# A column roll from memory to memory: both rows of a DMA engine in one transfer, and rings that take blocks in turn

## The chip, the core and the metric

The kernel runs on one core of a Trainium2 chip. The metric is the device time of one execution in microseconds (us); the time of a kernel is the median of its runs. The core has 16 DMA engines that all its DMA queues share, and five instruction engines. Three of these issue DMAs here: SP (SyncE) and ACT (ScalarE), each with a hardware ring, and POOL (GpSimd), with a software queue.

## The reference

```python
def setup_inputs():
    return {"x": np.random.randn(8192, 8192).astype(np.float32), "shift": 100}

def reference(x, shift):
    return np.roll(x, shift, axis=1)
```

Each of 8192 rows of 8192 float32 numbers (32 KB) is turned to the right by 100 places. Column c of the output is column c - 100 of the input; the first 100 columns of the output are the last 100 of the input. Nothing is computed: 268 MB are read and 268 MB are written.

## The kernel before

With `s = 100`, the kernel rounds the shift up to `a = 128` columns and cuts each row in two. The long part, output columns 128 to 8191, comes from input columns 28 to 8091. It goes from memory to memory in one step (line 36). The short part, output columns 0 to 127, goes through the core's own memory (lines 48 to 68).

The long part is cut into 256 blocks of 32 rows (lines 27 to 36). A block is seen as `e = 16` pairs of rows with `j = 2` rows in each, so that DMA engine e is meant to handle the neighbouring rows 2e and 2e + 1 of a block. For every block the kernel starts one DMA with the rows j = 0 on SP's ring and one with the rows j = 1 on ACT's ring. A DMA holds 16 pieces, one for each engine, and a piece is 8064 numbers, 32256 bytes. In the last eight blocks the columns are cut at `mid = 4096`, and each ring gets two DMAs per block, with pieces of 3968 and 4096 numbers. Each ring carries 248 + 16 = 264 DMAs.

The framework that schedules the program gives each ring four completion semaphores in turn. The order of instructions with their waits shows it: the first four DMAs of a ring wait for nothing, and each later one waits until the DMA four places ahead of it has landed in full, from all 16 engines. So a ring has at most four DMAs in flight. SP and ACT have no other work.

The short part is done in 16 groups of 512 rows. POOL loads each group with three DMAs (lines 60, 61 and 64), DVE copies the pieces into place (lines 62 and 65), and at the end POOL stores the 16 groups (line 68). POOL has eight completion semaphores in turn, so it has at most eight DMAs in flight. No row of the output is written twice and nothing in the long part waits for the short part or the other way round; they share the 16 DMA engines and the memory.

Of the kernel before, what the change touches and what calls it, by code (L numbers as in the profile page):

```python
# [1 line left out]

# [4 lines left out]


@with_exitstack
def kernel(  # L10
    ctx: ExitStack,
    tc: tile.TileContext,
    x: bass.AP,
    shift: int,
    out: bass.AP,
):
    nc = tc.nc
    n_rows, n_cols = x.shape
    s = shift % n_cols
    a = -(-s // 128) * 128  # L20
    g = a - s
    P = nc.NUM_PARTITIONS
    engines = [nc.sync, nc.scalar]
    n_chunks = 16
    rows = n_rows // n_chunks

    xm = x.rearrange("(c e j) w -> c j e w", e=16, j=2)
    om = out.rearrange("(c e j) w -> c j e w", e=16, j=2)
    if a < n_cols:
        blocks = n_rows // 32  # L30
        mid = (a + n_cols) // 256 * 128
        for c in range(blocks):
            parts = ((a, mid), (mid, n_cols)) if c >= blocks - 8 and a < mid else ((a, n_cols),)
            for j in range(2):
                for lo, hi in parts:
                    engines[j].dma_start(out=om[c, j, :, lo:hi], in_=xm[c, j, :, lo - s:hi - s])
    if a == 0:
        return

    if a > 512:  # L40
        for i in range(n_chunks):
            r = slice(i * rows, (i + 1) * rows)
            nc.gpsimd.dma_start(out=out[r, :s], in_=x[r, n_cols - s:])
            if g > 0:
                nc.gpsimd.dma_start(out=out[r, s:a], in_=x[r, :g])
        return

    Q = 4
    n_st = n_rows // (P * Q)
    reads = ctx.enter_context(tc.tile_pool(name="reads", bufs=n_st))  # L50
    heads = ctx.enter_context(tc.tile_pool(name="heads", bufs=n_st))
    xt = x.rearrange("(k p q) c -> k p q c", q=Q, p=P)
    ot = out.rearrange("(k p q) c -> k p q c", q=Q, p=P)
    tiles = []
    for k in range(n_st):
        t = reads.tile([P, Q - 1, a], x.dtype)
        h = heads.tile([P, Q, a], x.dtype)
        lead = bass.AP(tensor=x.tensor, offset=(k * P * Q + 1) * n_cols - s,
                       ap=[[Q * n_cols, P], [n_cols, Q - 1], [1, a]])
        nc.gpsimd.dma_start(out=t[:], in_=lead, single_packet=True)  # L60
        nc.gpsimd.dma_start(out=h[:, Q - 1, :s], in_=xt[k, :, Q - 1, n_cols - s:], single_packet=True)  # L61
        nc.vector.tensor_copy(h[:, :Q - 1, :s], t[:, :, :s])  # L62
        if g > 0:
            nc.gpsimd.dma_start(out=h[:, 0, s:], in_=xt[k, :, 0, :g], single_packet=True)  # L64
            nc.vector.tensor_copy(h[:, 1:, s:], t[:, :, s:])  # L65
        tiles.append(h)
    for k, h in enumerate(tiles):
        nc.gpsimd.dma_start(out=ot[k, :, :, :a], in_=h[:], single_packet=True)  # L68


# [1 line left out]
_INS = ['x', 'shift']  # L72
_OUTS = [((8192, 8192), 'float32')]

_NUMBERS = {'shift': 100}


# [26 lines left out]
```

## Time and profile before

| | |
|---|---|
| time before, median of 3 runs | 827.04 us (826.43 to 828.41) |
| the profiled execution, its own time | 825.38 us |
| its span, first to last instruction | 823.6 us |
| busy: DVE, POOL | 7.8 us (1%), 41.1 us (5%) |
| moved by the DMA engines | 272.71 MB, mean 331 GB/s |
| packets of the DMA engines | 20229, of them 9472 under 512 B |
| DMAs of line 36, per ring | 248 of 504 KB, 8 of 256 KB, 8 of 248 KB |

The page cuts the span into 40 slices. A digit is the share of the slice in tenths in which the 16 DMA engines were busy on average (9 is 90% or more), and below it stand the GB/s that they moved. A queue's line gives its packets, its megabytes and the time of its packets as a share of 16 engines' time. A line for DMA issues gives the number of DMAs, the KB of each, and the median time from issue to landing. In the table of windows, a row has the stretch, its length, the busy time of the engines that worked, the granted clock, the share in which the DMA engines were busy, and GB/s. A line of waits has the total time waited, the number of waits and the longest.

### The profile page before, as it was taken

The page shows a single profiled execution, that of the slowest core. Times are in us where ns is not written, and L with a number is a line of the kernel's source. Part 1 is how long each engine was busy: PE and PEld are TensorE (multiplying, and loading weights), DVE is VectorE, ACT ScalarE, POOL GpSimd, SP SyncE. Part 2 cuts the span into 40 slices and gives each one's busy share as a digit, 9 for nine tenths or more (in the row PEclk, how much of TensorE's full clock was granted, in tenths as well). Part 3 has the DMA queues.
Part 4 walks back from the last instruction along what each step waited for, and adds up shares of the span by engine and source line. Part 5 has one row for each costly group of instructions (what it writes and reads, how often), then busy time and mean ns, then how long its engine had stood idle before and what let it go on. Part 6 is the DMA issues. An engine that isn't in the chain of part 4 may idle for free. (4 is left out here: it accounts for less than half of the span.)

```text
span 823.6 us, 689 instructions
## 1 busy us (share of the span) xinstructions
DVE 7.8 (1%) x32; POOL 41.1 (5%) x68
## 2 busy tenths in 40 slices
DVE  0000000000000000000000000000000000000000
POOL 3111111211100000000000000000000000000000
DMA  9999999999999999999999999999999999999998
GB/s 300 345 338 345 325 338 340 332 344 359 341 341 345 338 337 323 332 332 321 329 331 331 324 329 331 332 326 329 332 326 329 336 323 337 320 335 337 321 312 302
DMA packets 20229, 272.71 MB, mean 331 GB/s; under 512 B 9472, under 2 KB 9728, under 8 KB 11776
## 3 DMA queue, kind: packets, MB, share of 16 engines
q1 hardware_dynamic: 8448, 132.14, 47.8%
q10 hardware_dynamic: 8448, 132.14, 46.7%
q0 software_dynamic: 3328, 8.39, 4.7%
q14 instruction: 5, 0.04, 0.0%
HBM read 268.44 MB, written 268.44 MB: 652 GB/s over the span
## 5 line engine op out<-in xcount | busy, mean ns | idle before, releaser
L68 POOL DMA_DIRECT2D out_dram<-h x16 | 11.4, 712 | 83.1 <-DMA out_dram<-h 49.6
L60 POOL DMA_DIRECT2D t<-in_x_dram x16 | 12.1, 758 | 32.5 <-DMA h<-in_x_dram 31.6
L64 POOL DMA_DIRECT2D h<-in_x_dram x16 | 8.6, 539 | 80.4 <-DMA t<-in_x_dram 80.4
L61 POOL DMA_DIRECT2D h<-in_x_dram x16 | 8.9, 558 | 20.8 <-DMA h<-in_x_dram 20.8
L62 DVE COPY h<-t 128x300 f32<-128x300 f32 x16 | 5.9, 368 | 179.7 <-DMA t<-in_x_dram 179.7
L65 DVE COPY h<-t 128x84 f32<-128x84 f32 x16 | 3.2, 201 | 0.0
L85 POOL MEMSET const-float32-0.0<- 128x1 f32 x1 | 0.1, 99 | 0.2 <-issue 0.2
L85 POOL MEMSET const-bfloat16-1.0<- 128x1 bf16 x1 | 0.1, 101 | 0.0
L85 POOL MEMSET const-uint8-127<- 128x1 uint8 x1 | 0.1, 99 | 0.0
L85 POOL MEMSET const-float32-1.0<- 128x1 f32 x1 | 0.1, 98 | 0.0
## 6 DMA issues: line engine op xcount, KB each, us to landing
out_dram<-in_x_dram ACTq DMA_DIRECT2D x248, 504.0 KB, 12.6
out_dram<-in_x_dram SPq DMA_DIRECT2D x248, 504.0 KB, 12.6
out_dram<-h POOLq DMA_DIRECT2D x16, 256.0 KB, 64.9
t<-in_x_dram POOLq DMA_DIRECT2D x16, 192.0 KB, 31.6
out_dram<-in_x_dram ACTq DMA_DIRECT2D x8, 256.0 KB, 6.0
out_dram<-in_x_dram SPq DMA_DIRECT2D x8, 256.0 KB, 5.9
out_dram<-in_x_dram ACTq DMA_DIRECT2D x8, 248.0 KB, 6.1
out_dram<-in_x_dram SPq DMA_DIRECT2D x8, 248.0 KB, 6.1
```

The lines of the kernel that those rows point to most:

```text
L60: nc.gpsimd.dma_start(out=t[:], in_=lead, single_packet=True)
L61: nc.gpsimd.dma_start(out=h[:, Q - 1, :s], in_=xt[k, :, Q - 1, n_cols - s:], single_packet=True)
L62: nc.vector.tensor_copy(h[:, :Q - 1, :s], t[:, :, :s])
L64: nc.gpsimd.dma_start(out=h[:, 0, s:], in_=xt[k, :, 0, :g], single_packet=True)
L65: nc.vector.tensor_copy(h[:, 1:, s:], t[:, :, s:])
L68: nc.gpsimd.dma_start(out=ot[k, :, :, :a], in_=h[:], single_packet=True)
L85: nc = _bacc.Bacc("TRN2", target_bir_lowering=False, num_devices=1)
```

## The change

Up to block 247, a block goes in one DMA on one ring: 32 pieces, both rows of each engine. Even blocks go on SP's ring and odd blocks on ACT's. In the last eight blocks, each ring carries one DMA per block with one whole piece per engine, SP those with j = 0 and ACT those with j = 1; the cut at `mid` is gone. The order of instructions on the engines shows 124 DMAs of 32 x 8064 and then 8 of 16 x 8064 on each ring, 132 in all. The four semaphores in turn per ring remain. The instructions of POOL and DVE are the same as before.

```diff
-    xm = x.rearrange("(c e j) w -> c j e w", e=16, j=2)
-    om = out.rearrange("(c e j) w -> c j e w", e=16, j=2)
+    xm = x.rearrange("(c e j) w -> c e j w", e=16, j=2)
+    om = out.rearrange("(c e j) w -> c e j w", e=16, j=2)
     if a < n_cols:
         blocks = n_rows // 32
-        mid = (a + n_cols) // 256 * 128
         for c in range(blocks):
-            parts = ((a, mid), (mid, n_cols)) if c >= blocks - 8 and a < mid else ((a, n_cols),)
-            for j in range(2):
-                for lo, hi in parts:
-                    engines[j].dma_start(out=om[c, j, :, lo:hi], in_=xm[c, j, :, lo - s:hi - s])
+            if c < blocks - 8:
+                engines[c % 2].dma_start(out=om[c, :, :, a:], in_=xm[c, :, :, a - s:n_cols - s])
+            else:
+                for j in range(2):
+                    engines[j].dma_start(out=om[c, :, j, a:], in_=xm[c, :, j, a - s:n_cols - s])
```

## The prediction

> **What bounds the kernel now.** I read the page first: its slices, its DMA queues and its memory line.
>
> ```profile
> DMA  9999999999999999999999999999999999999998
> GB/s 300 345 338 345 325 338 340 332 344 359 341 341 345 338 337 323 332 332 321 329 331 331 324 329 331 332 326 329 332 326 329 336 323 337 320 335 337 321 312 302
> q1 hardware_dynamic: 8448, 132.14, 47.8%
> q10 hardware_dynamic: 8448, 132.14, 46.7%
> q0 software_dynamic: 3328, 8.39, 4.7%
> HBM read 268.44 MB, written 268.44 MB: 652 GB/s over the span
> ```
>
> The 16 DMA engines are busy from the first slice to the last, and DVE and POOL work for 1% and 5% of the span. q1 and q10 are the rings of SP and ACT, q0 is POOL's. A ring shows 8448 packets for 264 DMAs: 264 x 16 = 4224 pieces and as many 4-byte packets that report completion.
>
> Second, the DMA view of the middle, 300 to 700 us, where POOL is done, and the instructions of line 36 in the same stretch:
>
> ```profile
> q1 hardware_dynamic: 4077, 65.78, 50.3%
> q10 hardware_dynamic: 4077, 65.75, 49.5%
> out_dram<-in_x_dram SPq DMA_DIRECT2D x128, 504.0 KB, 12.6
> out_dram<-in_x_dram ACTq DMA_DIRECT2D x128, 504.0 KB, 12.6
> ```
> ```profile
> L36 SPq DMA_DIRECT2D out_dram<-in_x_dram x128: 509/510/510, 299.9 to 699.6; - x128
> DMA to landing us min/median/max: 11.6/12.6/13.5
> ```
>
> The shares sum to 99.8%, and the software and instruction queues bring it to 99.9%: no engine goes hungry. One piece with its completion packet takes 0.503 x 16 x 400 us / (4077 / 2) = 1.58 us. A ring has four DMAs in flight (its fifth waits for the first), and 4 x 2 rings x 1.58 = 12.6 us, the landing time exactly. So a DMA's landing time is queueing, and a fixed cost in it would be covered by the seven others.
>
> Third, SP's own waits in that stretch:
>
> ```profile
> SPq L36 <- DMA out_dram<-in_x_dram: 335.3, 128, 3.5
> ```
>
> SP issues for 128 x 0.51 = 65 us and waits 335 us of 400: issuing has five times the room it needs.
>
> What is full then? From 0 to 250 us the DMA view gives 38.45 + 38.65 MB on the two rings and 7.20 MB on POOL's. A ring's byte uses memory twice (read and write), a POOL byte once: (154.2 + 7.2) MB / 250 us = 646 GB/s. In the middle it is 131.53 x 2 / 400 = 658 GB/s. The rate of the DMAs falls from 337 to 329 GB/s when POOL's share goes, while the memory's flow stays within 2%. I take the memory's flow as the bound; the engines are busy because packets wait inside them.
>
> Last, the end, in windows (length, DVE, POOL, clock, DMA share, GB/s):
>
> ```profile
> 600.00:780.00 180.00, 0.00 (x0) 0.00 (x0) 1.00 1.00 330
> 780.00:800.00 20.00, 0.00 (x0) 0.00 (x0) 1.00 0.97 322
> 800.00:810.00 10.00, 0.00 (x0) 0.00 (x0) 1.00 0.91 318
> 810.00:824.00 14.00, 0.00 (x0) 0.00 (x0) 1.00 0.81 269
> ```
>
> The halved pieces run here. Four half-size DMAs per ring are less cover, so 3% and 9% idle appear, and the last 14 us lose 14 x (1 - 269/330) = 2.6 us against the middle's rate.
>
> **The change part by part.**
>
> *Half the DMAs in the bulk.* Each ring issues 124 DMAs of 32 pieces and 8 of 16, 132 in place of 264; bytes are the same. An engine handles 264 completion packets in place of 528 over both rings, and its 32 half pieces of the last blocks become 16 whole ones. What is a completion packet worth? The last stage shows it, since there every 16 KB has one in place of every 32 KB. By elapsed time, 780 to 800 us gives 32256 x 16 / 322 = 1603 ns per 32256 bytes of an engine, the middle 32256 x 16 / 330 = 1564 ns: 39 ns for one more completion, if the whole loss is put on it. By busy time it is 1603 x 0.97 = 1555 ns against 1564: nothing, or below nothing. So the saving is 0 to 264 x 39 ns = 10.3 us. I take 0, by the busy-time row: the 3% is idle time, which a dearer packet would not make.
>
> *Deeper rings.* Four DMAs in flight are now eight pieces per ring and engine in place of four. It can only remove idle time; the middle has 0.1% of it: 0 to 780 x 0.001 = 0.8 us. I take -0.4.
>
> *Rows dealt differently.* Before, the rings work on odd and even rows of one block, 32 KB apart; after, on neighbouring blocks, 1 MB apart. Order on a ring is row 2e, then 2e + 1, of its block for engine e, if the queue deals rows out as the diff's view says. No row depends on another, and nothing else is queued on SP or ACT. Every engine still holds one packet at a time in its own region of memory, and engines already stand at different points of different blocks. I price it at 0 and keep both signs: the slices after POOL's end run from 320 to 338 GB/s apart from the last two, so a bulk of 780 us at 330 could move by 780 x (330/320 - 1) = +24 us or 780 x (330/338 - 1) = -18 us. These are extremes of single slices, so I put the likely part near a third of either, +8 and -6.
>
> *POOL's queue.* It shares the engines. If an engine's turn on a ring is now two pieces long, POOL's transfers (31.6 us for the loads, 64.9 for the stores) take up to twice as long, and its chain ends near 2 x 257 = 514 us in place of 257 (where the chain of waits has its last store). The rings' remaining 310 us hide it: price 0. Without that cover, each further us would count in full.
>
> *Start.* The first DMA of each ring takes 0.51 us to issue for 16 pieces; for 32 it takes 0.51 to 1.02 us. At the start alone this can delay an engine: 0 to +0.5, I take +0.2. Later the 335 us of waiting cover it.
>
> *End.* The last eight blocks return to the sizes of today's middle, so the 780 to 810 us stretches regain 20 x (1 - 322/330) + 10 x (1 - 318/330) = 0.8 us. Against that the last pieces are twice as long. If half of the 2.6 us lost at the very end is engines waiting for the last piece of another, it doubles: +1.3; if none is, 0; if all is, +2.6. Net +0.5 (from -0.8 to +1.8).
>
> Sum: 0 - 0.4 + 0 + 0 + 0.2 + 0.5 = +0.3 us. The profiled execution took 825.38 us (span 823.6 and 1.8 around it), so 825.7; the median of the three runs lies 1.66 higher, hence 827.3. That is no change: 0.3%, or 2.5 us, is about what a measurement of this kernel can tell from none.
>
> **The rivals.**
>
> *A completion or a fixed time per DMA costs what the end suggests (faster).* For it: the rate falls as soon as the DMAs are halved, at 780 us. Against: the loss is idle time and not busy time. Price up to -10.3 us: about 817. It decides if the piece time falls below 1.58 us in the middle. The Trainium skill (DMA: Bandwidth & Descriptors, the tables of "Measured" and "Rules for kernel authors") asks for 1 MiB per DMA and gives a fixed 2.0 us for each; were it not hidden, I estimate from it 264 x 2.0 / 8 in flight = 66 us saved, which would make the sum 761. The middle's 99.9% busy share speaks against that in full. Chance 0.17.
>
> *Two rings a megabyte apart meet in the memory (slower).* Engine e's row in block c and in block c + 1 differ by 2^20 bytes, and the rings start in step. For it: the memory's 658 GB/s is what binds, so any worse order of addresses shows in full. Against: the engines are not in step after the first pieces (landings vary from 11.6 to 13.5 us). Price: to the lowest slices, up to +24 us; likely a third, about 835. It decides once the piece time in the middle exceeds 1.60 us. The same page (section "Latency and other measured facts") reports copies losing rate where lock-stepped rows lie at a large power of two: 207 GB/s at 512 KiB, 164 at 2 MiB, of 214. Taken whole, an estimate by it, for the spacing of 1 MiB between these two, is +26 to +238 us. No row here shows such a loss at today's spacings. Chance 0.18.
>
> *Engines drift further apart and the end pays (slower).* With eight pieces in a ring a quick engine may run 8 x 2 x 1.58 = 25 us ahead in place of 12.6. If so, the last DMAs wait for the slowest engine as the present end does, twice as long: another 0.19 x 14 = 2.7 us on top of the forecast, 830. Against: the landings' spread of 2 us in the middle shows no engine running away. It decides once the share falls under 0.8 over more than the last 14 us. Chance 0.07.
>
> *The change does not do what it says.* If one engine got rows in another order, or the queue cut DMAs into today's units, landing would stay at 12.6 us and the time at 827. Chance 0.03.
>
> **How the numbers follow.** The forecast has 0.52; its unknown terms (-0.8 to +1.8 at the end, 0.8 for depth, 0.5 at the start, and small moves of the memory's rate) leave 0.42 within 0.3%, and 0.05 on each side. An order of rows that suits the memory better (to -18 us, likely 821) has 0.03. Within 0.3%: 0.42 + 0.03 (the last rival) = 0.45. Faster by over 0.3%: 0.05 + 0.17 + 0.03 = 0.25. Slower: 0.05 + 0.18 + 0.07 = 0.30. Range: down to 819, short of the first rival's full price, and up to 837, past the second's likely price; about one in ten is left out at each end.
>
> **What the next profile would show.** Right: 4224 completion packets fewer (8448 per ring becomes 6208 or so: 124 x 48 + 8 x 32), landing near 25 us in the middle and 12.6 in the last blocks, the middle at 328 to 332 GB/s, and no dip before the last 14 us. The middle above 334 GB/s would mean that completions cost time; below 326, that the new order of rows hurts; a long thin end, that drift does. POOL's chain ending past 350 us would show turns of two pieces.

## The result and the profile after

The changed kernel takes 839.25 us (median of 5 runs, 836.5 to 839.98) against 827.93 us (826.43 to 829.52) for the kernel before on the same chip: 1.0136 of it, 95% interval 1.0116 to 1.0156. It is slower by 11.3 us, outside the range of 819 to 837 us and on the side that had a chance of 0.30. The profiled execution is the median one, 839.25 us, with a span of 837.5 us: 13.9 us more than the span of before. (Of the kernel before, the profiled execution took 825.38 us, less than its median, so the spans differ by more than the medians do.)

The page of the changed kernel, its slices, queues and memory line:

```profile
DMA  9999999999999999999999999999999999999986
GB/s 302 324 341 332 325 330 327 331 337 333 320 340 342 329 339 340 341 337 339 335 323 319 324 331 322 324 328 328 327 322 322 325 328 324 331 320 330 330 280 239
...
q10 hardware_dynamic: 6208, 132.13, 46.7%
q1 hardware_dynamic: 6208, 132.13, 46.6%
q0 software_dynamic: 3328, 8.39, 4.8%
...
HBM read 268.44 MB, written 268.44 MB: 641 GB/s over the span
```

6208 packets per ring are 4096 pieces and 2112 completions: the change does what it says. The memory's flow is 641 in place of 652 GB/s, and the last two slices fall to 280 and 239 GB/s (before: 312 and 302). The DMA view and line 33's instructions from 300 to 700 us, and SP's waits there:

```profile
q10 hardware_dynamic: 2989, 64.26, 48.9%
q1 hardware_dynamic: 2999, 64.61, 48.8%
q0 software_dynamic: 927, 2.99, 2.0%
```
```profile
DMA to landing us min/median/max: 24.1/25.8/27.3
```
```profile
SPq L33 <- DMA out_dram<-in_x_dram: 365.6, 62, 6.8
```

Landing doubled, as eight pieces per ring and engine must make it. POOL still has work at 300 us; its loads land after 48.5 us (before 31.6). The windows of the end (length, DVE, POOL, clock, DMA share, GB/s):

```profile
600.00:780.00 180.00, 0.00 (x0) 0.00 (x0) 1.00 0.99 326
780.00:800.00 20.00, 0.00 (x0) 0.00 (x0) 1.00 0.99 323
800.00:810.00 10.00, 0.00 (x0) 0.00 (x0) 1.00 0.87 297
810.00:824.00 14.00, 0.00 (x0) 0.00 (x0) 1.00 0.78 253
824.00:837.50 13.50, 0.00 (x0) 0.00 (x0) 1.00 0.61 220
```

The 13.9 us have two places. **The end:** idle time of an average engine after 780 us is 0.01 x 20 + 0.13 x 10 + 0.22 x 14 + 0.39 x 13.5 = 9.9 us, before it was 0.03 x 20 + 0.09 x 10 + 0.19 x 14 = 4.2 us: 5.7 us more. **The middle:** after 780 us the changed kernel still moves 15.9 MB (the four rates by their lengths), the kernel before 13.4 MB. So it is 2.5 MB behind when the end begins, some 8 us at 326 GB/s. As the memory's flow from 100 to 760 us (rings' megabytes twice, POOL's once, by the DMA view of each): before (2 x 213.53 + 6.10) MB / 660 us = 656 GB/s, after (2 x 210.68 + 6.76) / 660 = 649 GB/s, 1.1% less. The engines' shares of that stretch sum to 99.9% before and 99.4% after, so only half of it is idle engines.

The trace also records when each engine adds its one to a DMA's completion semaphore. That gives what no landing time shows, how far the engines are apart within a DMA. Medians over the large DMAs issued from 300 to 700 us, in us:

| kernel | pieces in flight per ring and engine | issue to first engine | first to last engine | last engine behind the mean | issue to landing |
|---|---|---|---|---|---|
| before | 4 | 7.1 | 5.5 | 3.9 | 12.6 |
| changed | 8 | 6.8 | 18.8 | 16.0 | 25.8 |

The first engine of a DMA in the changed kernel is done 6.8 us after the issue. Its two pieces and the other ring's two take 4 x 1.57 = 6.3 us, about the whole 6.8 us, so it had hardly anything else queued, while the last engine has the ring's whole depth before it. In the kernel before, 7.1 us are twice what its own and the other ring's single piece take (3.2 us), so even the first engine had other pieces queued.

### The profile page after: what moved, and what is told of

It is laid out like the page before. It is cut to its first block, busy times and chain, and to the rows that moved or that the text cites. A ratio compares the mean times of both kernels' runs of the same rounds, so it can differ in the third digit from the quotient of the medians.

```text
span 837.5 us, 425 instructions
## 1 busy us (share of the span) xinstructions
DVE 7.8 (1%) x32; POOL 41.1 (5%) x68
## 3 DMA queue, kind: packets, MB, share of 16 engines
q10 hardware_dynamic: 6208, 132.13, 46.7%
q1 hardware_dynamic: 6208, 132.13, 46.6%
## 6 DMA issues: line engine op xcount, KB each, us to landing
out_dram<-in_x_dram ACTq DMA_DIRECT2D x124, 1008.0 KB, 25.8
t<-in_x_dram POOLq DMA_DIRECT2D x16, 192.0 KB, 48.5
```

## The experiments

The experiments ran on other chips, where the kernel before takes 816 to 826 us; ratios are to the kernel before on the same chip. All but two ran on chips where it takes 816 to 818 us, "that kind of chip" below; the last two forms with two DMAs in flight ran where it takes 825.5 us. "Spread" is the time from the first to the last engine of a DMA, as in the table above. Theory of **depth**: the engines drift apart until the rings' depth is filled, and the drift is paid at the end. Theory of **row order**: which rows lie in one DMA, or on the two rings at one time, costs in the memory.

### One piece per DMA, rings in turn

```diff
-                engines[c % 2].dma_start(out=om[c, :, :, a:], in_=xm[c, :, :, a - s:n_cols - s])
+                for j in range(2):
+                    engines[c % 2].dma_start(out=om[c, :, j, a:], in_=xm[c, :, j, a - s:n_cols - s])
```

(In this and in other runs with two DMAs of one ring in a row, the last eight blocks are issued in pairs, so that each ring keeps its own four semaphores.)

> The rings take blocks in turn as in the changed kernel, but each DMA holds one piece per engine, so a ring holds four pieces per engine as before; the last eight blocks are in whole pieces. Theory of depth (engines drift apart until the rings' depth is filled, and both the middle's rate and the end pay for it): 825 to 830 us, landing near 12.6 us, the middle at 329 to 331 GB/s, the DMA share under 0.9 only in the last 15 us. Theory of row order (two rings a megabyte apart meet in the memory): 834 to 838 us, the middle at 326 GB/s or less.

Measured: 1.0003 (0.9991 to 1.0016). The spread is 5.1 us, the last engine 3.7 us behind the mean, landing 12.5 us. The windows of the end:

```profile
600.00:770.00 170.00, 0.00 (x0) 0.00 (x0) 1.00 1.00 332
...
790.00:800.00 10.00, 0.00 (x0) 0.00 (x0) 1.00 0.98 329
800.00:810.00 10.00, 0.00 (x0) 0.00 (x0) 1.00 1.03 342
```

(In a window as short as 10 us a share can come out a little above 1.) No loss until the last 7 us of a span of 816.9. So rings that take blocks in turn, a megabyte apart, cost nothing by themselves, and neither do whole pieces in the last eight blocks.

### Two pieces per DMA, the old rows on each ring

```diff
-                engines[c % 2].dma_start(out=om[c, :, :, a:], in_=xm[c, :, :, a - s:n_cols - s])
+                if c % 2 == 0:      # xp, op: "(d b e j) w -> d j e b w", b=2, e=16, j=2
+                    for j in range(2):
+                        engines[j].dma_start(out=op[c // 2, j, :, :, a:], in_=xp[c // 2, j, :, :, a - s:n_cols - s])
```

> SP keeps the rows j = 0 and ACT the rows j = 1, as before, but a DMA of the first 248 blocks holds the pieces of two neighbouring blocks, two per engine, so a ring holds eight pieces per engine; the last eight blocks are as in the changed kernel. Theory of depth: 836 to 841 us, landing near 25.7 us, the DMA share under 0.9 from about 25 to 35 us before the end. Theory of row order: 826 to 831 us with the middle at 329 to 331 GB/s, though landing is 25 us all the same.

Measured: 1.0084 (1.0059 to 1.0110). Spread 18.1 us, last engine 14.4 us behind the mean. Its windows:

```profile
600.00:770.00 170.00, 0.00 (x0) 0.00 (x0) 1.00 1.00 334
...
790.00:800.00 10.00, 0.00 (x0) 0.00 (x0) 1.00 0.79 248
800.00:810.00 10.00, 0.00 (x0) 0.00 (x0) 1.00 0.83 297
```

The middle is hardly disturbed (a flow of 662 GB/s from 100 to 760 us, against 664 of the kernel before in its repetition, below) and the end is nearly as poor as the changed kernel's. With the old rows, deeper rings alone bring the drift and cost 0.8%, somewhat less than the 836 us expected and less than the changed kernel.

### Two short pieces per DMA

```diff
-                engines[c % 2].dma_start(out=om[c, :, :, a:], in_=xm[c, :, :, a - s:n_cols - s])
+                for lo, hi in ((a, mid), (mid, n_cols)):
+                    engines[c % 2].dma_start(out=om[c, :, :, lo:hi], in_=xm[c, :, :, lo - s:hi - s])
```

> The changed kernel's blocks on rings in turn and two pieces per engine and DMA, but each block's columns are cut in half, so that a DMA holds two pieces of 16 KB per engine and a ring as many bytes as before. Theory of depth: 825 to 830 us, landing near 12.6 us. Theory of row order: 834 to 838 us. A third theory, that two pieces behind one completion are themselves dealt badly: 834 us or more, with the two sizes in its favour if landing stays at 12.6 us.

Measured: 1.0066 (1.0048 to 1.0085). Landing is 12.7 us and the end is short, as depth says, yet the kernel is slower: a miss for the theory of depth as the only one. The flow from 100 to 760 us is 659 GB/s, against 664 of the kernel before on that kind of chip (its repetition, below). The halved pieces are a second difference here; the run with two large DMAs in flight, below, loses as much with whole ones.

### The old end behind the new middle

The last eight blocks as in the kernel before, the rest as changed.

> The changed kernel with the last eight blocks of the kernel before (halved pieces, two DMAs per ring and block). Theory of depth: the drift at block 248 is what costs, and smaller pieces behind it win back 2 us at most: 835 to 841 us, with the share under 0.9 for more than 25 us at the end. Theory that the coarser last pieces cost: 829 to 834 us, the end as short as before.

Measured: 1.0154 (1.0101 to 1.0207), with runs from 823.2 to 834.4 us. Halved pieces at the end win nothing back: where the rings become shallow, from 790 to 800 us, the DMA share falls to 0.59 and the rate to 205 GB/s.

### The changed kernel and the kernel before, again

> The changed kernel, unaltered, on the chip that also runs the next three. Both theories: 1.010 to 1.017 of the kernel before on this chip. It settles what the first comparison left unclear: if the middle (400 to 770 us) runs at the rate of the kernel before's here, the whole cost lies at the end; if it is 1% lower, the deep rings cost in the middle too.

> The kernel before, unaltered, for a trace on this chip beside the others: 0.998 to 1.002. If its middle (400 to 770 us) runs at 331 to 334 GB/s like the kernel with single pieces on rings in turn, the changed kernel's lower middle of the first pair belongs to that pair of executions; if at 336 GB/s or more, the deep rings cost in the middle.

> The changed kernel, unaltered, on the same chip as the three above: 1.011 to 1.016 by both theories.

Measured: changed 1.0138 (1.0099 to 1.0178) and 1.0101 (1.0068 to 1.0135), before 0.9992 (0.9971 to 1.0014). The engines' idle time after 760 us, summed from the windows as above, is 10.6 us in the first of the two changed ones and 4.9 us in the kernel before: 5.7 us more, as in the first pair (here the two traces are of two chips of that kind). The middle is less clear. The two profiled executions of the changed kernel are the fastest of their runs (825.5 of 825.5 to 829.8, 820.1 of 820.1 to 829.0) and show a flow of 662 and 664 GB/s against 664 before. So the lower middle is not in every execution. The changed kernel's runs scatter by up to 9 us, those of the repeated kernel before by 6 us (814.2 to 819.8).

### Deep first, shallow later

```diff
-            if c < blocks - 8:
+            if c < blocks // 2:
```

> The first 128 blocks as in the changed kernel (eight pieces per ring and engine), the last 128 in one piece per engine and DMA (four). Theory of depth: the drift is paid where the rings become shallow, so a dip of some 25 to 35 us with the DMA share at 0.8 to 0.9 stands near 400 us, the end is as short as with single pieces throughout, and the time is still 1.004 to 1.010 of the kernel before. Theory that only an end that is too short for the drift costs: no dip in the middle and 0.998 to 1.003.

Measured: 1.0076 (1.0051 to 1.0102). The windows around the place where the depth changes:

```profile
400.00:410.00 10.00, 0.00 (x0) 0.00 (x0) 1.00 1.00 341
410.00:420.00 10.00, 0.00 (x0) 0.00 (x0) 1.00 0.96 341
420.00:430.00 10.00, 0.00 (x0) 0.00 (x0) 1.00 0.86 276
430.00:440.00 10.00, 0.00 (x0) 0.00 (x0) 1.00 0.95 343
```

The dip has moved to the middle with the change of depth: where the rings become shallow, the spread falls from 17.4 us (DMAs issued from 300 to 400 us) to 4.9 us (400 to 500 us). The dip is smaller than expected (0.4 + 1.4 + 0.5 = 2.3 us of idle time), so it is not the whole 0.76%. But a longer shallow stretch at the end does not take the cost away. The rows of the first half, whose cost shows below, are a likely part of the rest; this run does not separate them.

### Four pieces per DMA

```diff
-                engines[c % 2].dma_start(out=om[c, :, :, a:], in_=xm[c, :, :, a - s:n_cols - s])
+                if c % 2 == 0:      # xq, oq: "(d e j) w -> d e j w", e=16, j=4; d = c // 2
+                    engines[d % 2].dma_start(out=oq[d, :, :, a:], in_=xq[d, :, :, a - s:n_cols - s])
```

> As the changed kernel, but a DMA of the first 248 blocks holds four pieces per engine (64 rows, two blocks), so 16 pieces per ring and engine are in flight. Theory of depth: the engines' spread follows the depth again, about 44 us of a landing time near 51 us, and the end takes two to three times the loss of the changed kernel: 1.02 to 1.04 of the kernel before. Theory that the drift has a bound of its own near 18 us: about the changed kernel's time, 1.010 to 1.017.

Measured: 1.0273 (1.0237 to 1.0309). Landing is 50.6 us, the spread 37.5 us, the last engine 28.3 us behind the mean. The slices of the last 40 us, one us each (798 to 838 us):

```profile
DMA  3932231194960000097092999599598995000000
GB/s 129 452 129 97 97 129 65 65 323 194 323 226 32 32 0 32 32 290 258 32 484 97 452 516 355 194 419 419 194 387 290 323 331 226 32 32 0 32 0 0
```

From 810 to 815 us at most one engine of 16 works: one piece of 32 KB per us or so is started, while the rings wait for DMAs that are not finished. From 832 us the same is seen again. At depths of 4, 8 and 16 pieces (the run with single pieces, the changed kernel's first repetition, this run) the last engine is 3.7, 14.7 and 28.3 us behind the mean, and the times are 1.000, 1.014 and 1.027. Idle time after 760 us is 4.9 (kernel before), 10.6 and 20.9 us. In these three the drift grows with the depth. The end accounts for 16.0 of the 23.2 us between this span and that of the kernel before (838.4 and 815.2 us); the rest lies before it, and four neighbouring rows in one DMA are a second difference here.

### Which engine is behind

```diff
+                if 48 <= c and c % 16 >= 14:   # shortened: k = 1, 2, 4, 8 in turn
+                    engines[c % 2].dma_start(out=m[:k], in_=x[32 * c:32 * c + k, 0:1])
```

> The changed kernel with a very small DMA behind every eighth large DMA of a ring from block 62 on: one number to each of 1, 2, 4 or 8 partitions of the core's memory, which nothing uses. Such a DMA stands in the rings of 1, 2, 4 or 8 engines alone, behind the large one, so the moment at which it lands tells how far these engines are. Theory that one fixed engine lags: each size always stands at the same distance from the large DMA's last engine; the size that holds the laggard lands with it, the others 10 to 18 us before. If the laggard is none of the eight, all four sizes land 10 us or more before the last engine. Theory that engines drift at random and change places: the distances of one size scatter from 0 to 18 us. Time 1.008 to 1.018 of the kernel before.

Measured: 1.0124 (1.0092 to 1.0155). The spread is 11.1 us and the last engine 8.3 us behind the mean, less than without the small DMAs. From the semaphores' records, from 300 us on, the last of the small DMA's engines against the last engine of the large one ahead of it, in us (minus is earlier):

| engines | SP's ring | ACT's ring |
|---|---|---|
| 1 | -7.3, -5.3 | -9.6, -10.9 |
| 2 | -6.9, -7.3, -7.0 | -8.5, -7.6, -7.0 |
| 4 | +2.3, +1.5, +1.7 | -5.1, -4.9, -3.7 |
| 8 | +1.9, +1.6 | +2.2, +3.6 |

A small DMA stands one turn behind the large one, so a positive number marks an engine that is the last or level with it. The distances of each k repeat to within 2 us, so this engine is fixed for hundreds of us. On SP's ring it is the third or fourth, on ACT's one of the fifth to eighth; it does not change places at random. (Taken that a DMA to k partitions uses the first k engines, as the Trainium skill says in DMA: Bandwidth & Descriptors, "Why a DMA increments its semaphore by 16 and not by 1"; the semaphores' records agree in the number: a small DMA to k partitions leaves k records of engines; which engines they are, no run here shows.) That the two rings have different last engines was expected by neither theory. Why these are behind was not found.

### Without the short part

The long part of both kernels alone.

> The changed kernel without the short part: columns 0 to 127 are left out, and POOL and DVE do nothing. Theory that POOL's transfers hold one engine back: the spread of the engines stays under 8 us, the end is short, and the time is within 0.4% of the next kernel's. Theory that the rings' depth alone lets the engines drift: spread near 18 us again, 1.009 to 1.015 of the next kernel's time.

> The kernel before without the short part: columns 0 to 127 are left out. The 8.4 MB of POOL's share are 3.1% of the bytes, but count once in the memory where the long part counts twice: 0.96 to 0.985 of the kernel before. Both theories: landing near 12.6 us and a spread under 7 us.

Measured: 0.9965 (0.9946 to 0.9983) and 0.9838 (0.9804 to 0.9871), so the changed long part takes 814.65 / 803.65 = 1.0137 of the old one, worked out from the medians. The time is what the theory of depth expected, but its reason is not: the spread is 7.9 us (before: 5.7) and not near 18, the last engine is 5.2 us behind the mean, and the first engine of a DMA is done 17.3 us after the issue, so it still had work queued. The idle time after 760 us is 6.1 us against 4.7, which is 1.4 of the 10.7 us between the two spans (812.6 and 801.9 us). So two signs of the theory of POOL came true (a spread under 8 us and a short end), and only the time speaks against it. POOL's traffic is not the cause of the whole loss, but in this execution without it the engines drift much less, and deep rings alone did not make a spread of 18 us.

The rest, some 9 us, lies before the end: 657 against 663 GB/s of flow from 100 to 760 us, and more at the start. The changed long part first, then the old one (length, POOL, clock, DMA share, GB/s):

```profile
20.00:100.00 80.00, 0.00 (x0) 1.00 1.00 318
100.00:200.00 100.00, 0.00 (x0) 1.00 0.99 323
```
```profile
20.00:100.00 80.00, 0.00 (x0) 1.00 1.00 331
100.00:200.00 100.00, 0.00 (x0) 1.00 1.00 332
```

The rate is lowest while the engines are still level (a spread of 3.0 us for DMAs issued in the first 100 us), so this loss is not the drift's.

### Two large DMAs in flight, four forms

A DMA of one number behind each large one takes two of the ring's four semaphores.

```diff
                 engines[c % 2].dma_start(out=om[c, :, :, a:], in_=xm[c, :, :, a - s:n_cols - s])
+                m = marks.tile([1, 1], x.dtype)
+                engines[c % 2].dma_start(out=m[:], in_=x[32 * c:32 * c + 1, 0:1])
```

Four runs have this; the first has the changed kernel's rows, and the others say what a DMA's 32 rows are.

> The changed kernel, but behind every DMA of the first 248 blocks comes a DMA of one number into the core's memory on the same ring (nothing uses the number). These take two of the ring's four completion semaphores, so that only two of the large DMAs, four pieces per engine, are in flight on a ring. Theory of depth: landing near 12.6 us, the spread between engines back to about 6 us, the end short, 0.998 to 1.006 of the kernel before. Theory that two pieces behind one completion cost in themselves: still 1.010 or more, with the end as long as in the changed kernel.

> Two large DMAs in flight per ring, held so by DMAs of one number behind them as in the run with two in flight, but the two pieces of a DMA are the same row of two neighbouring blocks, SP with j = 0 and ACT with j = 1. Theory that neighbouring rows in one DMA cost: 0.998 to 1.004 of the kernel before. Theory that two large DMAs in flight are too few: 1.006 to 1.012, as with neighbouring rows.

> Two large DMAs in flight per ring, held so by DMAs of one number. Of four neighbouring rows SP's ring takes the first two in a DMA and ACT's the last two, so a DMA is 16 groups of two neighbouring rows and no single run of 32. Theory that an engine's neighbouring rows in one DMA cost: 1.006 to 1.012 of the kernel before, the middle (400 to 760 us) at 327 to 329 GB/s. Theory that the run of 32 rows is what costs: 0.997 to 1.003, the middle at 331 to 334 GB/s.

> Two large DMAs in flight per ring, held so by DMAs of one number. Of 64 rows SP's ring takes the even ones in one DMA and ACT's the odd ones: a run of 32 rows with one stride, in which no two are neighbours. Theory that neighbouring rows in one DMA cost: 0.997 to 1.003 of the kernel before. Theory that the run of 32 rows is what costs: 1.006 to 1.012, the middle at 327 to 329 GB/s.

| a DMA's rows | rings | ratio (95% interval) |
|---|---|---|
| an engine's two neighbouring rows, one run of 32 rows | in turn by blocks | 1.0090 (1.0057 to 1.0122) |
| the same row of two blocks, 1 MB apart | side by side | 0.9987 (0.9975 to 0.9999) |
| two neighbouring rows, 16 groups | side by side | 1.0025 (1.0012 to 1.0039) |
| one run of 32 rows, every other row | side by side | 0.9999 (0.9988 to 1.0010) |

Landing is 12.5 to 12.7 us in all four. The first two, on the same kind of chip, from 400 to 760 us:

```profile
400.00:760.00 360.00, 0.00 (x0) 0.00 (x0) 1.00 0.99 329
```
```profile
400.00:760.00 360.00, 0.00 (x0) 0.00 (x0) 1.00 0.99 332
```

Large DMAs and half the completions are harmless in themselves: the second run has both and is no slower than the kernel before. With the changed kernel's rows the middle is 1% slower at the same share, with no deep ring (spread 3.8 us against 5.3 us). Neighbouring rows in one DMA cost 0.25% with rings side by side; a run of 32 rows costs nothing. The full 0.9% is seen only with neighbouring rows and rings in turn together. The last two were expected to differ in the middle; both ran at 328 GB/s there, and no trace of the kernel before was taken on their kind of chip, so for them the times alone count.

### Deep rings, one change of rows each

```diff
# rows apart, rings in turn by pairs of blocks: "(d b e j) w -> d j e b w", b=2
+                engines[d % 2].dma_start(out=op[d, j, :, :, a:], in_=xp[d, j, :, :, a - s:n_cols - s])
# neighbouring rows, rings side by side: "(d e r j) w -> d r e j w", r=2, j=2
+                engines[r].dma_start(out=op[d, r, :, :, a:], in_=xp[d, r, :, :, a - s:n_cols - s])
```

> Deep rings (two pieces per engine and DMA, four DMAs in flight) that take turns, here by pairs of blocks; the two pieces of a DMA are the same row of two neighbouring blocks, 1 MB apart, not two neighbouring rows. Theory that neighbouring rows in one DMA cost: the cost of the deep end alone, 1.006 to 1.010 of the kernel before, the middle (400 to 760 us) at 332 GB/s or more. Theory that taking turns costs with deep rings: 1.012 to 1.017, the middle lower.

> Deep rings that work side by side as before: of four neighbouring rows of an engine, SP's ring takes the first two in one DMA and ACT's the last two. So the two pieces of a DMA are neighbouring rows, but the rings do not take turns by blocks. Theory that neighbouring rows in one DMA cost: 1.012 to 1.017 of the kernel before, like the changed kernel. Theory that taking turns costs: 1.006 to 1.010.

Measured: 1.0056 (1.0032 to 1.0079) with rows apart, 1.0089 (1.0067 to 1.0112) with neighbouring rows. Turns alone add nothing to the deep end's cost. The intervals overlap, so this pair alone does not settle what neighbouring rows add. The middles point the same way without settling it: 333 and 331 GB/s.

Seven of the profiled executions, put side by side, show what the idle time at the end goes by. How far the last engine is behind is the median over the large DMAs issued from 600 to 760 us:

| execution | pieces in flight per ring and engine | last engine behind the mean, us | idle time after 760 us, us |
|---|---|---|---|
| kernel before, again | 4 | 4.1 | 4.9 |
| rows apart, rings in turn | 8 | 3.7 | 4.5 |
| changed, without the short part | 8 | 6.5 | 6.1 |
| changed, second repetition | 8 | 11.7 | 7.8 |
| changed, first repetition | 8 | 14.7 | 10.6 |
| changed, first pair | 8 | 16.3 | 10.1 |
| four pieces per DMA | 16 | 28.3 | 20.9 |

The four others with deep rings fit in (7.9 us behind and about 5.5 us idle with the small DMAs, 10.4 and 10.4 with neighbouring rows side by side, 12.0 and 9.6 with the old end, 14.9 and 9.3 with the old rows). At one depth the end costs nothing or 6 us, as the last engine is level or far behind. The depth only bounds how far it can fall behind. (The execution with rows apart was the fastest of its runs, 816.2 of 816.2 to 825.5 us.)

## Why the prediction was wrong

**The bound**, memory flow with busy engines, was not tested by itself. In its favour, the kernel before has the same flow with the short part and without it (664 and 663 GB/s). But the step "no engine goes hungry, so depth can only help" looked at the average of 16 engines. A share of 99.9% does not say how far the engines are apart.

**Completions** at 0, and not at 10.3 us: right. With half of them and the old rows the time is 0.9987. The reading of the price was not right: the halved pieces start to move at 794.6 us, so most of what moves from 780 to 800 us (159 whole pieces, 82 halved) is as in the middle, and the dip there is no price of completions; the 0.8 us credited to the end rests on the same reading. The first rival, a fixed cost per DMA, falls, and with it the estimate of 66 us from the Trainium skill: DMAs of 0.5, 1 and 2 MB gave 1.000, 1.014 and 1.027. (The Trainium skill gives the fixed 2.0 us in DMA: Bandwidth & Descriptors, "Anatomy of one DMA", as a fit for DMAs that GpSimd issues, and not in the two tables named.)

**Deeper rings** at -0.4 us: the failed step. "It can only remove idle time" is wrong: in the first pair and in the first repetition there is 5.7 us more of it at the end with the deeper rings. Depth also bounds how far the quickest engine can leave the last one behind; in these executions that bound is nearly reached, in the one without the short part it is not. Why an engine lags, and why it lagged less without POOL's traffic, is open. The evidence given against drift ("the landings' spread of 2 us in the middle shows no engine running away") was a misreading: a landing is the last engine's, and says nothing about the first. The first engine was already 5.5 us ahead.

**The end** at +0.5 us (-0.8 to +1.8): mis-sized. It costs 5.7 us, in two pairs of traces, in idle time. The reason given (longer last pieces) is not it: the run with single pieces has the same last pieces and 1.0003. The third rival had the mechanism and its sign (the share is 0.78 and 0.61 over the last 27.5 us), with a price of 2.7 us and a chance of 0.07.

**Rows dealt differently** at 0: the second step that failed; right for rings in turn alone (1.0003), wrong for the form that the change has. In the first pair the middle lost some 8 us, just the likely price given to the second rival, but not for its reason: rings a megabyte apart cost nothing while a DMA held one piece. The rule on large powers of two that the Trainium skill states in DMA: Bandwidth & Descriptors, "Latency and other measured facts", did not show at this spacing. What the runs tie the loss to is neighbouring rows in one DMA with rings in turn, up to 0.9%. What the memory or the queues do with them is open, and so is why some executions of the changed kernel hardly show it.

**POOL** at 0: right for its own chain, which ends near 390 us (the chain of waits has its last long pieces at 369 and 379 us), past the 350 us named for longer turns, and before the 514 us of full doubling; the end of the kernel has none of it. That the engines drift less without its transfers was not foreseen. **Start**: line 33's DMAs of 32 pieces take SP 510 ns to issue, as those of 16 did, and the first 20 us run at 295 GB/s (before 297); nothing shows the 0.2 us that were taken.

## What to carry to other kernels

When equal work is dealt to engines that do not keep the same pace, the queue's depth bounds how far they drift apart, and the drift is paid where the queue runs out; give queues the depth that keeps the engines busy and no more (here four pieces, of 12.6 us). Ask for the first and the last engine of a DMA, not for its landing time or the mean busy share. To cut the number of DMAs without that cost, halve the DMAs in flight when doubling their size, and watch which rows lie in one DMA.

## What was not expected of the hardware

One engine stays the last for hundreds of us, a different one on each ring (the run with the small DMAs). The last engine is 16 us behind the mean with a landing time of 25.8 us, and 28 us with 50.6 us at twice the depth, but only 5 us with 25.3 us when POOL moves nothing. Without the short part, the changed kernel is 4% slower from 20 to 100 us than the kernel before (318 against 331 GB/s), while its engines are still level; the cause is open. A DMA of 32 pieces takes SP the same 510 ns to issue as one of 16. On the chip that ran both, two kernels with deep rings scattered more from run to run (820.1 to 829.0 and 816.2 to 825.5 us) than the kernel before and the one with two large DMAs in flight (815.0 to 819.0 and 814.0 to 817.9 us).

No version measured here that does the whole work beats the kernel before by more than 0.3%; two large DMAs in flight with the old rows come nearest (0.9987).
